# A decoder trunk: low weight parts built by an accumulating DMA, another order in the value product, a finer cut of the last columns

## The chip, the cores and the metric

The kernel runs on one core of a Trainium2 chip. The core has a tensor engine for matrix products (PE; its weight loads are shown apart as PEld), a vector engine (DVE), a scalar engine (ACT), GpSimd (POOL) and a sync engine (SP) that issues most DMAs. Matrix products read SBUF and write PSUM, eight banks of 128 x 512 fp32 each. The metric is the device time of one execution in microseconds (us).

## The reference

One layer (DEPTH = 1) on 512 tokens of width 1024. What matters here:

```python
h = rmsnorm(x, norm_mix_pre[l])
proj = h @ w_in[l]
...
y_b = swa_mixer(s_q, s_k, s_v, swa_sinks[l]) @ w_branch_swa[l]     # sliding-window attention, 128-token blocks
...
x = x + rmsnorm(merged @ w_out[l], norm_mix_post[l])
h = rmsnorm(x, norm_ffn_pre[l])
f = conv_ffn(h, ffn_w_up[l], ffn_conv_w[l], ffn_conv_b[l], ffn_w_down[l])
x = x + rmsnorm(f, norm_ffn_post[l])

def conv_ffn(h, w_up, conv_w, conv_b, w_down):
    ...                                            # up (1024 -> 2 x 2816), causal depthwise conv, split
    return (jax.nn.gelu(gate, approximate=True) * val) @ w_down     # 2816 -> 1024
```

In `swa_mixer` each block of 128 queries reads its own and the previous block of keys; the value product is `einsum('bnhgqk,bnkhd->bnqhgd', p / denom, vw)`.

## The kernel before, in words

**Split products.** Almost every product is done on pairs: each fp32 matrix is split into a high part, rounded to the reduced format fp32r, and a low part, what is left. A product is then three matmuls into the same PSUM bank: high x high, high x low, low x high. Weights are split on the core. `load_raw` (L62) brings 128 x 1024 fp32 (512 KB) into a buffer `raw` (two of them) by a DMA of SP; `split` (L67) makes `whi` by a rounding copy on ACT (L68) and `wlo = raw - whi` on DVE (L69). There are four buffers each for `whi` and `wlo`, used in turn, so the split of a weight waits until PE is done with the weight four places earlier. `weight_order` lists all weights in the order of use, and `weight` (L95) starts the load of the weight `AHEAD` = 2 places on whenever it hands one out.

**Order on the engines.** Dependencies between instructions, and the waits that follow, are worked out by the framework when the program is built. It also orders the instructions of each engine: a list scheduler goes through them by the order in which they were written, with times that it supposes for each, and takes an instruction written later where an earlier one would not be ready. So an engine's order in the trace can differ from the order in the code, and it is fixed before the run.

**The value product** (`swa_b`, L404). For each of the four blocks of queries, eight heads of probabilities are transposed on PE into two banks (`pt`, one for each half `hh` of four heads). In block 0 ACT copies them (L414). In blocks 1 to 3 DVE multiplies each bank by two masks (L419), which gives the products for the previous and the own block of keys. Then PE multiplies with the values (L426) into one bank `po`: half 0 to partitions 0 to 63, half 1 to partitions 64 to 127, with `n` = 1 (block 0) or 2 matmuls for each half. These are fp32 and show as two records each.

**The down product.** After the up products, `ah` and `al` hold the activations' parts, 22 chunks of 128 rows. The output is 4 token tiles x 2 column halves = 8 banks `pd[t][n]`, all open at once. For chunks 0 to 17 the loop runs over chunks, tiles and halves: `d_mm` (L836) issues three matmuls for each half, 24 for a chunk. The last four chunks (18 to 21) are loaded ahead, their weights held in all four buffers, and are done output by output: for each tile, for each half, the 12 matmuls of the four chunks. As each half is done, ACT squares it with a running sum (`jkf`, L856), and DVE multiplies it by the norm's gain (`fg`, L858). After the second half `rstd_m2` (L121) works out the inverse root from the sum, DVE adds the result to the residual `x1` (L865), and SP stores it (L867).

Of the kernel before, what the change touches and what calls it, by code (L numbers as in the profile page):

```python
# [7 lines left out]
F32 = mybir.dt.float32  # L8
F32R = mybir.dt.float32r
I32 = mybir.dt.int32  # L10
AF = mybir.ActivationFunctionType
ALU = mybir.AluOpType
AX = mybir.AxisListType

P = 128
T = 512
D = 1024
KC = D // P
NT = T // P
DFF = 2816  # L20
NF = DFF // P
EPS = 1e-6
VC = 656
# [27 lines left out]
def kernel(ctx: ExitStack, tc: tile.TileContext, x, xT, w_first, w_tiles, w_v, w_br, w_out, w_up, w_down,  # L51
                      pool_w, wgu, small, sinks, g_mix_post, g_ffn_pre, g_ffn_post,
                      ident_in, sel_in, tri_in, lvl_mask_in, scan_mask_in, pool_rc_in, out):
    nc = tc.nc
# [16 lines left out]
    def new_w():  # L71
        return (wp.tile([P, 1024], F32R, tag="whi", name="whi", bufs=4),
                wp.tile([P, 1024], F32R, tag="wlo", name="wlo", bufs=4))

    def load_w(src, cols=1024):
        raw = load_raw(src, cols)
        hi, lo = new_w()
        split(raw, hi, lo, slice(0, cols))
        return hi, lo
# [3 lines left out]
    loaded = {}  # L83
    pos = {"next": 0, "used": 0}

    def prefetch(upto):
        while pos["next"] < min(upto, len(order)):
            k = order[pos["next"]]
            src = tabs[k[0]]
            for i in k[1:]:  # L90
                src = src[i]
            loaded[k] = load_w(src, VC if k[0] == "v" else 1024)
            pos["next"] += 1

    def weight(*key, ahead=AHEAD):  # L95
# [39 lines left out]
    def base_of(pool, ssq, tag):  # L135
        b = pool.tile([P, 1], F32, tag=tag, name=tag, bufs=2)
        nc.vector.tensor_scalar(b, ssq, 1.0 / D, EPS, op0=ALU.mult, op1=ALU.add)
        return b
# [108 lines left out]
    with tc.tile_pool(name="mp", bufs=1) as mp:  # L247
# [77 lines left out]
        for i in range(4):  # L325
            qf_ = t2([P, T], f"swa_qf{i}")
            nc.vector.scalar_tensor_tensor(out=qf_, in0=pq[i], scalar=0.125, in1=rstd_b, op0=ALU.mult, op1=ALU.mult)
            for e in range(2):
                a, z = half[e], half[1 - e]
# [4 lines left out]
        for e in range(2):  # L334
            a, z = half[e], half[1 - e]
# [9 lines left out]
        for half in range(2):  # L345
            pv = [psm.tile([P, T], F32, tag="mm", name=f"pv{half}_{t}") for t in range(NT)]
            for k2 in range(4):
                hi, lo = weight("v", half * 4 + k2)
                for t in range(NT):
                    for kk in range(2):  # L350
                        kc = k2 * 2 + kk
                        c = slice(kk * 328, (kk + 1) * 328)
                        tk = slice(t * P, (t + 1) * P)
# [8 lines left out]
        def swa_steps():  # L362
            yh, yl = ybr[1] = new_y("y_swa")
            blk = {}
            nc.vector.tensor_scalar(nsink, sink, -1.0, None, op0=ALU.mult)

            def swa_a(b):
                s = t4([P, 8, P], f"s{b}")
                own = slice(b * P, (b + 1) * P)
                prev = slice((b - 1) * P, b * P)  # L370
                for hh in range(2):
                    for i2 in range(2):
                        sc = psx.tile([P, 2, 2, P], F32, tag="mx", name=f"sc{b}_{hh}_{i2}")
                        for ii in range(2):
                            q = qs[hh][:, i2 * 2 + ii, own]
                            if b:
                                kk = ks[:, hh, :, (b - 1) * P : (b + 1) * P]
                                nc.tensor.matmul(sc[:, ii, :, :], q, kk[:, 0, :], start=True, stop=False)
                                nc.tensor.matmul(sc[:, ii, :, :], q, kk[:, 1, :], start=False, stop=True)
                            else:  # L380
                                nc.tensor.matmul(sc[:, ii, 1, :], q, ks[:, hh, 0, own], start=True, stop=False)
                                nc.tensor.matmul(sc[:, ii, 1, :], q, ks[:, hh, 1, own], start=False, stop=True)
                        sv = s[:, hh * 4 + i2 * 2 : hh * 4 + i2 * 2 + 2, :]
                        nc.scalar.copy(sv, sc[:, :, 1, :])
                        nc.vector.copy_predicated(sv, sel.unsqueeze(1).to_broadcast([P, 2, P]),
                                                  sc[:, :, 0, :] if b else neg.unsqueeze(2).to_broadcast([P, 2, P]))
                mx = mp.tile([P, 8], F32, tag="mxs", name="mxs", bufs=2)
                nc.vector.tensor_reduce(out=mx, in_=s, op=ALU.max, axis=AX.X)
                nm = mp.tile([P, 8], F32, tag="nm", name="nm", bufs=2)
                nc.vector.scalar_tensor_tensor(out=nm, in0=mx, scalar=-1.0, in1=nsink, op0=ALU.mult, op1=ALU.min)  # L390
                es = mp.tile([P, 8], F32, tag="es", name="es", bufs=2)
                nc.vector.tensor_add(es, sink, nm)
                nc.scalar.activation(es, es, AF.Exp)
                den = mp.tile([P, 8], F32, tag="den", name="den", bufs=2)
                for h in range(8):
                    nc.scalar.activation(s[:, h, :], s[:, h, :], AF.Exp, bias=nm[:, h : h + 1], accum_out=den[:, h : h + 1])
                nc.vector.tensor_add(den, den, es)
                rd = mp.tile([P, 8], F32, tag="rd", name="rd", bufs=2)
                nc.vector.reciprocal(rd, den)
                for h in range(8):  # L400
                    nc.vector.tensor_scalar(s[:, h, :], s[:, h, :], rd[:, h : h + 1], None, op0=ALU.mult)
                blk[b] = s

            def swa_b(b):  # L404
                s = blk.pop(b)
                po = psx.tile([P, 4, P], F32, tag="mx", name=f"po{b}")
                pts = []
                for hh in range(2):
                    pt = psx.tile([P, 4, P], F32, tag="mx", name=f"pt{b}_{hh}")
                    for i in range(4):  # L410
                        nc.tensor.transpose(pt[:, i, :], s[:, hh * 4 + i, :], ident)
                    if b == 0:
                        own = t2([P, 4, P], f"pT{b}")
                        nc.scalar.copy(own, pt)  # L414
                        pts.append((own,))
                    else:
                        two = t4([P, 2, 4, P], f"pT{b}_{hh}")
                        for j in range(2):
                            nc.vector.tensor_tensor(out=two[:, j, :, :], in0=pt,  # L419
                                                    in1=tri[:, j, :].unsqueeze(1).to_broadcast([P, 4, P]), op=ALU.mult)  # L420
                        pts.append((two[:, 0, :, :], two[:, 1, :, :]))
                for hh in range(2):
                    n = len(pts[hh])
                    for j in range(n):
                        vb = vv[:, b - n + 1 + j, V_SV + hh * 64 : V_SV + hh * 64 + 64]
                        nc.tensor.matmul(po[hh * 64 : hh * 64 + 64, :, :], vb, pts[hh][j], start=j == 0, stop=j == n - 1)  # L426
                bs = slice(b * P, (b + 1) * P)
                nc.scalar.copy(yh[:, :, bs], po)
                nc.vector.tensor_sub(yl[:, :, bs], po, yh[:, :, bs].bitcast(F32))

            swa_a(0)
            yield
            for b in range(NT):
                if b + 1 < NT:
                    swa_a(b + 1)
                    yield
                swa_b(b)
                yield
# [357 lines left out]
    with tc.tile_pool(name="fp", bufs=1) as fp:  # L796
# [39 lines left out]
        def d_mm(t, kc, wh, wl, ns_=(0, 1)):  # L836
            tk = slice(t * P, (t + 1) * P)
            for n in ns_:
                ns = slice(n * T, (n + 1) * T)
                nc.tensor.matmul(pd[t][n], ah[:, kc, tk], wh[:, ns], start=kc == 0, stop=False)  # L840
                nc.tensor.matmul(pd[t][n], ah[:, kc, tk], wl[:, ns], start=False, stop=False)  # L841
                nc.tensor.matmul(pd[t][n], al[:, kc, tk], wh[:, ns], start=False, stop=kc == NF - 1)  # L842

        for kc in range(NF - 4):
            wh, wl = weight("d", kc)
            for t in range(NT):
                d_mm(t, kc, wh, wl)
        wd = [weight("d", kc) for kc in range(NF - 4, NF)]
        for t in range(NT):
            ssf = fp.tile([P, 2], F32, tag="ssf", name="ssf", bufs=2)  # L850
            fg = []
            for n in range(2):
                for kc in range(NF - 4, NF):
                    d_mm(t, kc, *wd[kc - NF + 4], ns_=(n,))
                jk = fp.tile([P, T], F32, tag="t0", name="jkf", bufs=3)
                nc.scalar.activation(jk, pd[t][n], AF.Square, accum_out=ssf[:, n : n + 1])  # L856
                fgn = fp.tile([P, T], F32, tag="fg", name="fg", bufs=2)
                nc.vector.tensor_mul(fgn, pd[t][n], gpost[:, n * T : (n + 1) * T])  # L858
                fg.append(fgn)
                if n == 0:  # L860
                    fb = base_of(fp, ssf[:, 0:1], "fb")
            rf = rstd_m2(fp, ssf[:, 1:2], "rf", fb)
            for n in range(2):
                ns = slice(n * T, (n + 1) * T)
                nc.vector.scalar_tensor_tensor(out=x1[:, t, ns], in0=fg[n], scalar=rf, in1=x1[:, t, ns],  # L865
                                               op0=ALU.mult, op1=ALU.add)
                nc.sync.dma_start(out[t, :, ns], x1[:, t, ns])  # L867


def _layout(inputs):  # L870
# [89 lines left out]
```

## Time and profile before

| | |
|---|---|
| three runs | 800.25, 800.38, 802.51 us; median 800.38 |
| the profiled execution | 802.75 us, its span 801.0 |
| TensorE clock granted, mean | 0.997 |
| PE busy | 791.3 us of the span |
| DVE, ACT, POOL busy | 462.2, 328.3, 32.9 us |
| matmuls of the down product (L840 to L842) | 528, from 674.3 to 794.3 us of the span |
| DMA | 81.02 MB, 101 GB/s over the span |

Times in a trace are counted from the start of the span. A timeline row has the start, the length, the engine, the line of the code, the operation, what it writes and reads, and in brackets how long the engine was idle before it and who ended that. Matmuls are pipelined: a row's 0.39 us is the time of one through the array, and the next one starts 0.23 us after it. A row of the DMA table ends with the median time from issue to landing. A row of the waits has the sum, the number of times and the longest.

### The profile page before, as it was taken

Reading aid. Unit: us, or ns where it says so; the run is one execution under the profiler, and the core shown is the slowest. Engines: PE = TensorE matmul, PEld = TensorE weight load, DVE = VectorE, ACT = ScalarE, POOL = GpSimd, SP = SyncE. Lnnn points to the kernel's source line nnn. Section 1 sums busy time; section 2 is a strip of 40 time slices with the busy share of each in tenths; the row PEclk is TensorE's granted clock in tenths of the full one; section 3 lists DMA queues with packets and bytes.
Section 4 is the critical chain, followed back from the end, with each engine's and each line's share of the span. In section 5 each row is a group of like instructions: output and inputs, shape, how many; then the busy total and the mean of one; then the engine's idle time right before and its main releaser. Section 6 shows DMA issues by size and latency. Waiting matters only on the chain.

```text
span 801.0 us, 9610 instructions
## 1 busy us (share of the span) xinstructions
PE 791.3 (99%) x3748; PEld 655.1 (82%) x3748; DVE 462.2 (58%) x701; ACT 328.3 (41%) x541; POOL 32.9 (4%) x46
## 2 busy tenths in 40 slices
PE   9999999999999999999999999999999999999996
PEld 7899876778887888888889988888888888888885
DVE  6464676368786556545658666655655665221225
ACT  7354644473224342333445544444444444122132
POOL 0100000011413000000000100000000000000000
PEclk9999999999999999999999999999999999999999
DMA  9434211122224213222550233223223223223202
GB/s 339 128 107 138 74 62 60 65 79 79 79 93 132 80 52 106 92 93 79 174 194 28 93 117 106 92 93 105 97 89 105 101 84 106 98 86 106 104 29 105
DMA packets 24781, 81.02 MB, mean 101 GB/s; under 512 B 2976, under 2 KB 3248, under 8 KB 24736
## 3 DMA queue, kind: packets, MB, share of 16 engines
q1 hardware_dynamic: 23760, 77.83, 27.9%
q0 software_dynamic: 832, 2.58, 1.0%
q8 instruction: 29, 0.48, 0.2%
q14 instruction: 16, 0.13, 0.1%
q10 hardware_dynamic: 144, 0.00, 0.0%
HBM read 78.30 MB, written 2.10 MB: 100 GB/s over the span
## 4 chain that ended last, share of the span: by engine, by line
PE 97%; DVE 1%; ACT 1%; issue 1%; DMA 0%; DVEq 0%
PE up L104 10%; PE up L102 10%; PE up L103 10%; PE pj L102 8%; PE pj L104 8%; PE pj L103 8%; PE pd L841 5%; PE pd L842 5%; PE pd L840 5%; PE pq L195 3%; PE py L104 3%; PE py L103 3%; PE py L102 3%; PE pz L723 2%; PE pz L725 2%; PE pz L724 2%
## 5 line engine op out<-in xcount | busy, mean ns | idle before, releaser
L69 DVE TENSOR_TENSOR wlo<-raw,whi 128x1024 fp32r<-128x1024 f32 (+1 forms) x127 | 152.3, 1201 | 201.4 <-ACT whi L68 201.2
L68 ACT CAST whi<-raw 128x1024 fp32r<-128x1024 f32 (+1 forms) x127 | 131.0, 1032 | 232.8 <-PE pj L103 77.9
L102 PE MATMUL up<-h_hi,whi 128*128 128x512 f32 (+1 forms) x384 | 142.8, 372 | 0.0
L103 PE MATMUL up<-h_lo,whi 128*128 128x512 f32 (+1 forms) x384 | 142.6, 371 | 0.0
L104 PE MATMUL up<-h_hi,wlo 128*128 128x512 f32 (+1 forms) x384 | 142.6, 371 | 0.0
L102 PE MATMUL pj<-h_hi,whi 128*128 128x512 f32 x296 | 117.8, 398 | 0.0
L104 PE MATMUL pj<-h_hi,wlo 128*128 128x512 f32 x296 | 116.2, 392 | 0.0
L103 PE MATMUL pj<-h_lo,whi 128*128 128x512 f32 x296 | 115.8, 391 | 0.0
L103 PEld LDWEIGHTS up<-h_lo,whi 128*128 128x128 f32 x384 | 72.3, 188 | 12.6
L104 PEld LDWEIGHTS up<-h_hi,wlo 128*128 128x128 f32 x384 | 72.3, 188 | 12.5
L102 PEld LDWEIGHTS up<-h_hi,whi 128*128 128x128 f32 x384 | 72.3, 188 | 12.3
L841 PE MATMUL pd<-wlo,act_hi 128*128 128x512 f32 x176 | 68.6, 390 | 0.0
L842 PE MATMUL pd<-whi,act_lo 128*128 128x512 f32 x176 | 68.5, 389 | 0.0
L840 PE MATMUL pd<-whi,act_hi 128*128 128x512 f32 x176 | 68.3, 389 | 0.0
L104 PEld LDWEIGHTS pj<-h_hi,wlo 128*128 128x128 f32 x296 | 55.6, 188 | 14.7 <-issue 2.6
L102 PEld LDWEIGHTS pj<-h_hi,whi 128*128 128x128 f32 x296 | 55.8, 188 | 13.4 <-issue 2.6
L103 PEld LDWEIGHTS pj<-h_lo,whi 128*128 128x128 f32 x296 | 55.8, 188 | 12.1 <-issue 1.0
L841 PEld LDWEIGHTS pd<-wlo,act_hi 128*128 128x128 f32 x176 | 33.0, 188 | 7.2 <-DVE wlo L69 0.3
L840 PEld LDWEIGHTS pd<-whi,act_hi 128*128 128x128 f32 x176 | 33.0, 188 | 6.9
L842 PEld LDWEIGHTS pd<-whi,act_lo 128*128 128x128 f32 x176 | 33.0, 188 | 6.7
L817 ACT CAST act_hi<-t 128x512 fp32r<-128x512 f32 x22 | 13.7, 621 | 58.6 <-DVE t L816 58.6
L805 ACT ACTIVATE t<-up,small_sb 128x512 f32<-128x512 f32 x44 | 34.0, 774 | 0.0
(272 smaller groups left out, 1087.7 us busy)
## 6 DMA issues: line engine op xcount, KB each, us to landing
raw<-in_w_up_dram SPq DMA_DIRECT2D x44, 512.0 KB, 3.2
raw<-in_w_tiles_dram SPq DMA_DIRECT2D x37, 512.0 KB, 3.2
raw<-in_w_down_dram SPq DMA_DIRECT2D x22, 512.0 KB, 3.2
raw<-in_w_br_dram SPq DMA_DIRECT2D x12, 512.0 KB, 3.3
raw<-in_w_out_dram SPq DMA_DIRECT2D x8, 512.0 KB, 3.3
raw<-in_w_v_dram SPq DMA_DIRECT2D x8, 328.0 KB, 3.1
xT<-in_xT_dram SPq DMA_DIRECT2D x8, 256.0 KB, 4.5
wfr<-in_w_first_dram SPq DMA_DIRECT2D x8, 256.0 KB, 4.3
```

Of the source, the lines that this page charges most:

```text
L68: nc.scalar.copy(hi[:, c], raw[:, c])
L69: nc.vector.tensor_sub(lo[:, c], raw[:, c], hi[:, c].bitcast(F32))
L102: nc.tensor.matmul(ps, lh, rh, start=first, stop=False)
L103: nc.tensor.matmul(ps, lh, rl, start=False, stop=False)
L104: nc.tensor.matmul(ps, ll, rh, start=False, stop=last)
L195: nc.tensor.matmul(pq[i], w[:, kc, i * P : (i + 1) * P], h[:, kc, :], start=kc == 0 and n == 0, stop=kc == KC - 1 and n == 2)
L723: nc.tensor.matmul(pz[t][n], mh[:, kc % 4, tk], wh[:, ns], start=kc == 0, stop=False)
L724: nc.tensor.matmul(pz[t][n], mh[:, kc % 4, tk], wl[:, ns], start=False, stop=False)
L805: nc.scalar.activation(t0, ps, AF.Identity, bias=col(C_CB + i), scale=col(C_CW + 2 * 44 + i))
L840: nc.tensor.matmul(pd[t][n], ah[:, kc, tk], wh[:, ns], start=kc == 0, stop=False)
L841: nc.tensor.matmul(pd[t][n], ah[:, kc, tk], wl[:, ns], start=False, stop=False)
L842: nc.tensor.matmul(pd[t][n], al[:, kc, tk], wh[:, ns], start=False, stop=kc == NF - 1)
```

## The change

Three edits. The 22 down weights go through a new `load_w_acc`: ACT makes the high part, then writes the negated weight, rounded, into `wlo`; a DMA of POOL then reads the weight a second time from memory and adds it onto `wlo`. The subtraction on DVE is gone for them. In `swa_b` the loops over `hh` and `j` change places. The tail of the down product becomes a function over pieces of columns, two halves for tiles 0 to 2, and for the last tile one half and two quarters; the running base of the sum is a chain over the pieces, and `fg` is one tile of 1024 columns.

```diff
+    def load_w_acc(src):
+        raw = load_raw(src)
+        hi, lo = new_w()
+        nc.scalar.copy(hi, raw)
+        nc.scalar.activation(lo, raw, AF.Copy, scale=-1.0)
+        nc.gpsimd.dma_start(lo, src, accum_op=ALU.add)
+        return hi, lo
...
-            loaded[k] = load_w(src, VC if k[0] == "v" else 1024)
+            loaded[k] = load_w_acc(src) if k[0] == "d" else load_w(src, VC if k[0] == "v" else 1024)
...
-                for hh in range(2):
-                    n = len(pts[hh])
-                    for j in range(n):
+                n = len(pts[0])
+                for j in range(n):
+                    for hh in range(2):
                         vb = vv[:, b - n + 1 + j, V_SV + hh * 64 : V_SV + hh * 64 + 64]
                         nc.tensor.matmul(po[hh * 64 : hh * 64 + 64, :, :], vb, pts[hh][j], start=j == 0, stop=j == n - 1)
...
-                nc.tensor.matmul(pd[t][n], al[:, kc, tk], wh[:, ns], start=False, stop=kc == NF - 1)
+                nc.tensor.matmul(pd[t][n], al[:, kc, tk], wh[:, ns], start=False, stop=False)
...
-        for t in range(NT):
-            ssf = fp.tile([P, 2], F32, tag="ssf", name="ssf", bufs=2)
-            fg = []
-            for n in range(2):
+        def tail(t, pieces):
+
+            ssf = fp.tile([P, 4], F32, tag="ssf", name="ssf", bufs=2)
+            fg = fp.tile([P, D], F32, tag="fg", name="fg", bufs=2)
+            base = None
+            for k, (c0, c1) in enumerate(pieces):
+                n, cs = c0 // T, slice(c0, c1)
+                ps = pd[t][n][:, c0 - n * T : c1 - n * T]
+                tk = slice(t * P, (t + 1) * P)
                 for kc in range(NF - 4, NF):
-                    d_mm(t, kc, *wd[kc - NF + 4], ns_=(n,))
+                    wh, wl = wd[kc - NF + 4]
+                    for a, w in ((ah, wh), (ah, wl), (al, wh)):
+                        nc.tensor.matmul(ps, a[:, kc, tk], w[:, cs], start=False,
+                                         stop=a is al and kc == NF - 1, skip_group_check=c0 % T > 0)
                 jk = fp.tile([P, T], F32, tag="t0", name="jkf", bufs=3)
-                nc.scalar.activation(jk, pd[t][n], AF.Square, accum_out=ssf[:, n : n + 1])
-                fgn = fp.tile([P, T], F32, tag="fg", name="fg", bufs=2)
-                nc.vector.tensor_mul(fgn, pd[t][n], gpost[:, n * T : (n + 1) * T])
-                fg.append(fgn)
-                if n == 0:
-                    fb = base_of(fp, ssf[:, 0:1], "fb")
-            rf = rstd_m2(fp, ssf[:, 1:2], "rf", fb)
+                nc.scalar.activation(jk[:, : c1 - c0], ps, AF.Square, accum_out=ssf[:, k : k + 1])
+                if k < len(pieces) - 1:
+                    b = fp.tile([P, 1], F32, tag="fb", name="fb", bufs=4)
+                    nc.vector.tensor_scalar(b, ssf[:, k : k + 1], 1.0 / D, EPS if base is None else base,
+                                            op0=ALU.mult, op1=ALU.add)
+                    base = b
+                nc.vector.tensor_mul(fg[:, cs], ps, gpost[:, cs])
+            rf = rstd_m2(fp, ssf[:, k : k + 1], "rf", base)
             for n in range(2):
                 ns = slice(n * T, (n + 1) * T)
-                nc.vector.scalar_tensor_tensor(out=x1[:, t, ns], in0=fg[n], scalar=rf, in1=x1[:, t, ns],
+                nc.vector.scalar_tensor_tensor(out=x1[:, t, ns], in0=fg[:, ns], scalar=rf, in1=x1[:, t, ns],
                                                op0=ALU.mult, op1=ALU.add)
                 nc.sync.dma_start(out[t, :, ns], x1[:, t, ns])
+
+        for t in range(NT):
+            tail(t, ((0, 512), (512, 1024)) if t < NT - 1 else ((0, 512), (512, 768), (768, 1024)))
```

## The prediction

> **What bounds the kernel now.** I read the engine totals of the page first, then its chain of work, then busy time by stage, then single instructions around the one place where the tensor engine (PE) waits in the changed code.
>
> ```profile
> span 801.0 us, 9610 instructions
> PE 791.3 (99%) x3748; PEld 655.1 (82%) x3748; DVE 462.2 (58%) x701; ACT 328.3 (41%) x541; POOL 32.9 (4%) x46
> PE 97%; DVE 1%; ACT 1%; issue 1%; DMA 0%; DVEq 0%
> 10.00:20.00 10.00, 10.00 (x44) 8.17 (x44) 7.03 (x10) 7.92 (x12) 0.00 (x0) 1.00 1.01 392
> 674.00:772.40 98.40, 98.40 (x435) 81.48 (x435) 24.84 (x22) 20.28 (x20) 0.00 (x0) 1.00 0.26 91
> 772.40:794.40 22.00, 21.94 (x96) 17.57 (x95) 12.14 (x30) 8.06 (x20) 0.00 (x0) 1.00 0.19 72
> 794.40:801.00 6.60, 0.00 (x0) 0.00 (x0) 2.67 (x7) 0.96 (x3) 0.00 (x0) 0.86 0.21 79
> ```
>
> The third line is the chain that ended last: 97% PE. In the stage rows (columns: length, busy us of PE, weight loads, DVE, ACT, POOL, then clock, DMA share, GB/s) PE is busy all of the down stage's 98.4 us, DVE for only 24.84, ACT for 20.28, POOL for none. So taking 22 DVE subtractions away frees an engine that nothing waits for: it is worth nothing by itself. What counts is when a low weight part (wlo) is ready for PE, and the last 6.6 us, in which PE has nothing left.
>
> ```profile
> 756.09 1.05 ACT L68 CAST whi<-raw 128x1024 fp32r<-128x1024 f32 x1 [4.38 <-PE pd L842]
> ...
> 766.97 1.05 ACT L68 CAST whi<-raw 128x1024 fp32r<-128x1024 f32 x1 [4.38 <-PE pd L842]
> 772.41 1.05 ACT L68 CAST whi<-raw 128x1024 fp32r<-128x1024 f32 x1 [4.38 <-PE pd L842]
> 773.50 1.23 DVE L69 TENSOR_TENSOR wlo<-raw,whi 128x1024 fp32r<-128x1024 f32 x1 [4.22 <-ACT whi L68]
> 774.02 0.39 PE L842 MATMUL pd<-whi,act_lo 128*128 128x512 f32 x1
> 774.25 0.61 PE L840 MATMUL pd<-whi,act_hi 128*128 128x512 f32 x2
> 774.78 0.50 PE L841 MATMUL pd<-wlo,act_hi 128*128 128x512 f32 x1
> 775.11 0.39 PE L842 MATMUL pd<-whi,act_lo 128*128 128x512 f32 x1
> 775.34 0.40 PE L841 MATMUL pd<-wlo,act_hi 128*128 128x512 f32 x1
> PEld pd L841 <- DVE wlo L69: 0.3, 1, 0.3
> ```
>
> The casts come 5.44 us apart (766.97 to 772.41), each let go by the matmul that ends the use of the buffer four weights earlier. So PE spends 5.44 us on a weight, 24 matmuls of 0.227, and a cast starts three weights, 16.3 us, ahead of its use. The last weight (chunk 21) is the exception. The tail takes the first 512 columns of chunks 18 to 21 at once, so it wants wlo of chunk 21 after ten matmuls, at 774.47 if nothing waits (two steps of 0.227 after the 774.02 row), 2.1 us after its buffer came free at 772.4. Cast and subtraction take until 774.73, and PE waits 0.3 us, the stage's only wait. Two L840 stand in a row at 774.25, though one output takes L840, L841, L842 in turn: the second belongs to the other output, pulled forward into the gap. The order on an engine is thus not the written one; a scheduler fills a gap that it foresees. From 774.25 to 775.34 four steps took 1.09 us instead of 0.91: the wait costs 0.18.
>
> **The low parts by an accumulating DMA.** Removed: 22 DVE subtractions of 1.23 us. Added: 22 ACT instructions, 22 POOL issues, 22 transfers of 512 KB.
>
> ```profile
> L762 ACT ACTIVATE hn<-x 128x1024 f32<-128x1024 f32 x4 | 4.2, 1061 | 3.7 <-DVE x L757 3.6
> raw<-in_w_down_dram SPq DMA_DIRECT2D x22, 512.0 KB, 3.2
> x<-in_x_dram SPq DMA_DIRECT2D x4, 512.0 KB, 7.7
> 443.07 0.59 POOL L800 DMA_DIRECT2D g_ffn_post<-in_g_ffn_post_dram  x1 [193.04 <-ACT h_hi L773]
> 447.12 2.76 POOL L801 TENSOR_SCALAR g_ffn_post<-g_ffn_post 128x1024 f32<-128x1024 f32 x1 [3.46 <-DMA g_ffn_post<-in_g_ffn_post_dram]
> ```
>
> A scaled ACT copy of 1024 columns takes 1.06 us (L762's size), 22 x 1.06 = 23.3 us on an ACT that is 80% idle in the stage. A plain 512 KB transfer issued by POOL lands 447.12 - 443.07 = 4.05 us after its issue begins, the 0.59 of descriptor work included. No row shows an accumulating one. From below it is bounded by 4.05 (it must also read the tile that it adds to; nothing lets it move less), from above by the 7.7 us that 512 KB took on the full DMA of the start (x). I take the plain time and one more 512 KB of engine time: the stage's 0.26 share x 5.44 us = 1.41 us for each weight, so 4.05 + 1.41 = 5.46, nearest to the uncontended POOL row, since the stage leaves 74% of the DMA free.
>
> The Trainium skill, "Collectives: The Full Stack", section "The bandwidth ceiling: the fold count and why AG ≠ RS ≠ AR", says that an add in the DMA is slowed by its two source reads and not by the adding; by it the transfer part would about double. No run here shows that yet.
>
> Steady weights: cast 1.05, activation 1.06 and transfer 5.46 make 7.6 us (9.8 by the upper bound) against a lead of 16.3, so nothing; the cover goes only where a transfer takes over 14.2 us. The queues: ACT has only these in the stage; POOL has no work of its own there, so an accumulate that waits for ACT holds up only later ones; SP's next raw load waits for the second ACT read instead of the subtraction, 2.1 us instead of 2.3 after the cast began. DMA share: 0.26 now, 0.52 with a transfer priced as a raw one, 0.78 at double.
>
> The last weight is where it hurts. Its chain starts at 772.41 as before: 772.41 + 1.05 + 1.06 = 774.52, landing at 778.6 (plain), 780.0 (taken), 782.2 (upper). In written order PE wants it at 774.47. Chunk 20 has 5.44 us more and is wanted 0.68 sooner: hidden behind the same lateness. So wlo comes 5.5 us late (4.1 to 7.7). There is work for that gap: seven other outputs, each with ten matmuls that don't need this wlo, 70 x 0.227 = 15.9 us. Total PE work doesn't change, so what is filled costs nothing. How much is filled depends on the time that the scheduler supposes, which no row gives; ends are all and nothing. I take a gap planned for a plain transfer, since the 774.25 row shows lateness planned within one matmul: filled 4.1, left 1.41. **Cost +1.4 - 0.18 = +1.2 us** (0 - 0.18 to +7.5).
>
> **The last columns.** The last output's second half is cut into 256 + 256.
>
> ```profile
> 98.99 0.28 PE L378 MATMUL sc<-swa_k,swa_q 128*128 128x256 f32 x1
> ...
> 99.22 0.28 PE L378 MATMUL sc<-swa_k,swa_q 128*128 128x256 f32 x1
> L396 ACT ACTIVATE s<-s,nm 128x128 f32<-128x128 f32 x32 | 12.4, 389 | 7.8 <-DVE nm L390 7.8
> L856 ACT ACTIVATE jkf<-pd 128x512 f32<-128x512 f32 x8 | 4.8, 599 | 13.8 <-PE pd L842 13.8
> L858 DVE TENSOR_TENSOR fg<-pd,g_ffn_post 128x512 f32<-128x512 f32 x8 | 5.5, 690 | 8.3 <-ACT jkf L856 8.3
> L69 DVE TENSOR_TENSOR wlo<-raw,whi 128x1024 fp32r<-128x1024 f32 x119 | 145.8, 1225 | 192.1 <-ACT whi L68 191.9
> 795.10 0.69 DVE L858 TENSOR_TENSOR fg<-pd,g_ffn_post 128x512 f32<-128x512 f32 x1 [1.97 <-ACT jkf L856]
> 796.46 1.42 DVE L865 SCALAR_TENSOR_TENSOR x<-fg,rfr,x 128x512 f32<-128x512 f32 x2
> ```
>
> Matmuls of 256 columns start 0.115 us apart: 24 x 0.115 instead of 12 x 0.227 is +0.04. The last one takes 0.28 instead of 0.39: -0.11. The square on 256 columns saves 256 x (599 - 389)/384 ns = 0.14. The product saves (1225 - 690)/2 = 0.27. All stand in a row ahead of 796.46; what follows is unchanged. The first half's extra base and product run beside the second half's 1.4 us of matmuls. **-0.48 us**; bounds -0.5 and 0 (the square's fixed part could eat it).
>
> **The value product.** The order on two output halves changes from 0,0,1,1 to 0,1,0,1 in blocks 1 to 3; block 0 is the same.
>
> ```profile
> 95.92 1.41 PE po L426 x4
> 108.12 2.15 PE po L426 x6
> 112.99 1.00 PE po L426 x2
> 107.19 1.28 DVE L419 TENSOR_TENSOR pT<-pt,tri 128x512 f32<-128x512 f32 x2
> 108.46 0.68 DVE L419 TENSOR_TENSOR pT<-pt,tri 128x512 f32<-128x512 f32 x1
> 111.30 0.68 DVE L419 TENSOR_TENSOR pT<-pt,tri 128x512 f32<-128x512 f32 x1
> ```
>
> Each matmul is two records. Two records take 1.00 us, four that change halves once take 1.41, not 2: records of different halves overlap. More changes of half could overlap more. But the inputs decide: both inputs of half 0 are ready at 108.47, the first of half 1 at 109.14, the second at 111.98, and PE started that one only at 112.99, with other work between. When the first product ends (about 108.12 + 0.86 = 108.98), half 1 isn't ready and half 0's second input is, so the scheduler would choose the old order again. **0**, bounds -1.00 x 3 = -3.0 (the fourth product wholly overlapped) and +0.16 x 3 = +0.5 (PE waits from 108.98 to 109.14).
>
> **Sum.** 802.75 (the profiled execution) + 1.4 - 0.18 - 0.48 + 0 = 803.5. That execution lies 2.37 above the median, so I apply the difference, +0.74, to 800.38: **801.1 us**. What this measurement can tell from no change is 0.3%, 2.4 us: 798.0 to 802.8.
>
> **The rivals.**
> PE waits in full: the order isn't refilled, or for a much shorter time. For it: only one matmul was pulled forward so far. Against it: that was as much as was needed. Cost 4.1 to 5.5, less 0.66: 803.8 to 805.2. In the last stage row the granted clock averages 0.86 over 6.6 us without matmuls, so a long wait may also leave PE slow for some us, to 807. The Trainium skill, "TensorE: Matmul & The Clock Gate", Part 1, says that about 3.4 us idle bring the clock to half for as long again, an estimate of 1.7 us more here; the first matmul-free stretch that a trace of this case shows is the end.
>
> The accumulating transfer is slow in bulk. Beside a raw load's 1.41 us it must stay under 5.44 - 1.41 = 4.03 us of all engines, 2.9 plain ones; at four plain ones a weight takes 7.05 us, 22 x 1.6 = 35 us more, 836. The quiet 74% of the DMA speaks against it, the missing row leaves it open.
>
> Faster: PE's order changes in all three blocks, the fourth product overlaps each time, and the scheduler fills the last gap: 800.38 - 3.0 - 0.66 = 796.7. It decides from 1.8 us of gain on. Against it: the late fourth input, at 111.98.
>
> **How the numbers follow.** The forecast with its own range 799.7 (all filled) to 802.8: 0.48. Full wait: 0.22. The same mechanism with a remainder over 2.4 us after a slower transfer (about 804): 0.06. Bulk-bound: 0.09. Faster: 0.15. So faster 0.15, same 0.48, slower 0.37. The range 797.0 to 807.0 leaves out the bulk case and the best of the faster one.
>
> **What would show it.** Right: PE matmuls of other outputs between 774.4 and the landing of the last wlo, a wait of PE on a DMA of 1 to 2 us there and none at the other weights; DVE without L69 in the stage; PE's last matmul to the end about 0.5 us shorter; the product still in groups of 6 and 2. Wrong: PE waiting at every weight, a DMA share over 0.9 in the stage, or landings over 14 us after the issue; a single wait over 3 us with a clock below 1; or groups of 8 records.

## The result, and the profile after

The changed kernel took 804.0 us (median of 10 runs, 803.05 to 805.67), the kernel before 802.01 beside it on the same chip (10 runs, 800.25 to 802.63): a ratio of 1.0032, 95% interval 1.0022 to 1.0041. It is slower by about as much as this measurement can tell at all. The executions of the kernels that ran often fall in groups 1.6 to 1.9 us apart (before: near 798.7, 800.4 and 802.2), so besides the ratio I give the difference between like groups; for the change that is +2.9 us. Where that isn't enough, I count within a profiled execution from the end of the first product's 96 matmuls to the last instruction: 770.9 us before, 773.5 after, +2.6. Below, "profiled" with a signed number stands for this difference to the kernel before.

The profiled execution took 804.66 us. The head of its page, and below it the busy time by stage (length, busy us of PE, weight loads, DVE, ACT, POOL, then clock, DMA share, GB/s):

```profile
span 802.9 us, 9669 instructions
PE 790.9 (99%) x3760; PEld 654.5 (82%) x3760; DVE 435.6 (54%) x681; ACT 349.3 (44%) x565; POOL 52.1 (6%) x68
...
raw<-in_w_down_dram SPq DMA_DIRECT2D x22, 512.0 KB, 6.1
wlo<-in_w_down_dram POOLq DMA_DIRECT2D x22, 512.0 KB, 6.7
```

```profile
674.00:772.40 98.40, 98.40 (x436) 81.51 (x435) 2.88 (x4) 37.71 (x40) 15.68 (x18) 1.00 0.85 194
772.40:794.40 22.00, 19.87 (x92) 16.01 (x90) 10.82 (x29) 8.13 (x21) 0.87 (x1) 1.00 0.30 87
794.40:803.00 8.60, 1.69 (x12) 1.49 (x12) 2.95 (x9) 0.78 (x4) 0.00 (x0) 0.89 0.22 83
```

In the down stage DVE fell from 24.84 us to 2.88, ACT rose from 20.28 to 37.71, and PE is busy for all 98.40 us as before. The DMA share rose from 0.26 to 0.85. Nearly everything that the change did to the time comes after 772.4: there PE is busy for 19.87 of 22.00 us (21.94 before). The waits of PE's weight loads say where (us in total, times, longest):

```profile
PEld pd L869 <- DMA wlo<-in_w_down_dram: 2.0, 1, 2.0
PEld pd L869 <- DVE fg L878: 1.3, 1, 1.3
...
```

Two waits that count, each once. The first, in the timeline of the last weight (chunk 21):

```profile
771.19 1.06 ACT L79 ACTIVATE wlo<-raw 128x1024 fp32r<-128x1024 f32 x1 [3.44 <-PE pd L849]
771.22 0.39 PE L869 MATMUL pd<-whi,act_hi 128*128 128x512 f32 x1
...
772.16 1.03 ACT L78 CAST whi<-raw 128x1024 fp32r<-128x1024 f32 x1
...
772.54 0.87 POOL L80 DMA_DIRECT2D wlo<-in_w_down_dram  x1 [4.57 <-ACT wlo L79]
...
773.26 0.71 PE L869 MATMUL pd<-whi,act_hi 128*128 128x512 f32 x2
773.81 0.39 PE L869 MATMUL pd<-wlo,act_hi 128*128 128x512 f32 x1
...
775.64 0.39 PE L869 MATMUL pd<-whi,act_hi 128*128 128x512 f32 x1
777.66 0.50 PE L869 MATMUL pd<-wlo,act_hi 128*128 128x512 f32 x1 [1.63 <-DMA wlo<-in_w_down_dram]
778.00 0.39 PE L869 MATMUL pd<-whi,act_lo 128*128 128x512 f32 x1
```

ACT makes the negated copy first, then the cast. POOL issues the transfer at 772.54, and PE gets its result at 777.6, 5.06 us later. Ten matmuls after 771.22 PE would want it, at 773.49, so it is 4.1 us late. PE does ten matmuls of another output in that time, from the second one of the pair at 773.26 to 775.64, and then stands. From 775.87 to 777.66 is 1.8 us, and the first matmul after it costs 0.1 more.

The second wait, in the timeline of the last output (the first quarter's last matmul, DVE's product on it, the second quarter's first and last matmul):

```profile
793.62 0.28 PE L869 MATMUL pd<-whi,act_lo 128*128 128x256 f32 x1
794.57 0.41 DVE L878 TENSOR_TENSOR fg<-pd,g_ffn_post 128x256 f32<-128x256 f32 x1
795.04 0.38 PE L869 MATMUL pd<-whi,act_hi 128*128 128x256 f32 x1 [1.15 <-DVE fg L878]
...
796.46 0.28 PE L869 MATMUL pd<-whi,act_lo 128*128 128x256 f32 x1
```

The second quarter's columns are other columns than the first's, but they lie in the same PSUM tile and bank. PE doesn't start on them until ACT's square and DVE's product have read the first quarter: 1.3 us, and 0.1 for the restart. Before, the last matmul was this one:

```profile
793.95 0.39 PE L842 MATMUL pd<-whi,act_lo 128*128 128x512 f32 x1
```

From the start of the last matmul to the end of the span there are now 802.9 - 796.46 = 6.44 us, before 801.0 - 793.95 = 7.05: the shorter ending came, 0.61 us of it, and the wait ahead of it took more than twice that.

### The profile page after: what moved, and what is told of

Read it like the earlier page. It is cut to its first block, busy times and chain, and to the rows that moved or that the text cites. A ratio compares the mean times of both kernels' runs of the same rounds, so it can differ in the third digit from the quotient of the medians.

```text
span 802.9 us, 9669 instructions
## 1 busy us (share of the span) xinstructions
PE 790.9 (99%) x3760; PEld 654.5 (82%) x3760; DVE 435.6 (54%) x681; ACT 349.3 (44%) x565; POOL 52.1 (6%) x68
## 4 chain that ended last, share of the span: by engine, by line
PE 84%; issue 11%; POOL 2%; DVE 1%; DMA 1%; ACT 1%; DVEq 0%; POOLq 0%
PE up L110 10%; PE up L111 10%; PE up L112 10%; PE pj L112 8%; PE pj L110 8%; PE pj L111 8%; PE pq L203 3%; PE py L112 3%; PE py L111 3%; PE py L110 3%; PE pd L869 2%; POOL wlo L80 2%; PE pz L731 2%; PE pz L733 2%; PE pz L732 2%
## 5 line engine op out<-in xcount | busy, mean ns | idle before, releaser
L69 DVE TENSOR_TENSOR wlo<-raw,whi 128x1024 fp32r<-128x1024 f32 (+1 forms) x105 | 125.3, 1196 | 121.6 <-ACT whi L68 121.4
L68 ACT CAST whi<-raw 128x1024 fp32r<-128x1024 f32 (+1 forms) x105 | 107.8, 1027 | 153.1 <-PE pj L111 76.1
L848 PE MATMUL pd<-whi,act_hi 128*128 128x512 f32 x144 | 56.0, 389 | 0.0
L850 PE MATMUL pd<-whi,act_lo 128*128 128x512 f32 x144 | 56.0, 389 | 0.0
L849 PE MATMUL pd<-wlo,act_hi 128*128 128x512 f32 x144 | 56.0, 389 | 0.0
L79 ACT ACTIVATE wlo<-raw 128x1024 fp32r<-128x1024 f32 x22 | 23.3, 1059 | 59.3 <-PE pd L849 55.7
L80 POOL DMA_DIRECT2D wlo<-in_w_down_dram x22 | 19.2, 874 | 305.4 <-ACT wlo L79 305.4
L814 DVE SCALAR_TENSOR_TENSOR t<-up,small_sb,t 128x511 f32<-128x511 f32 x44 | 32.7, 744 | 11.3 <-ACT t L813 11.3
```

The costliest lines, as they stand in the source:

```text
L68: nc.scalar.copy(hi[:, c], raw[:, c])
L69: nc.vector.tensor_sub(lo[:, c], raw[:, c], hi[:, c].bitcast(F32))
L79: nc.scalar.activation(lo, raw, AF.Copy, scale=-1.0)
L80: nc.gpsimd.dma_start(lo, src, accum_op=ALU.add)
L814: nc.vector.scalar_tensor_tensor(out=t0[:, 1:], in0=ps[:, : T - 1], scalar=col(C_CW + 44 + i), in1=t0[:, 1:], op0=ALU.mult, op1=ALU.add)
```

## The experiments

Three kernels do one part of the change each, on the kernel before.

**The accumulating transfer alone.**

```diff
-            loaded[k] = load_w(src, VC if k[0] == "v" else 1024)
+            loaded[k] = load_w_acc(src) if k[0] == "d" else load_w(src, VC if k[0] == "v" else 1024)
```

> The kernel before with the accumulating DMA for the 22 down weights and nothing else of the change. Theory A (the last weight's low part lands about 1.9 us after PE has run out of pulled-forward matmuls, the other 21 are hidden): +1.7 to +1.9 us on before, ratio 1.0022, one PE wait on a DMA of about 2 us at chunk 21, none elsewhere. Rival B (the loaded DMA engines, 0.85 of the stage, cost the whole of the slowdown): +2.9 us, ratio 1.0036, with several PE or ACT waits spread over the stage.

802.61 us, ratio 1.0024 (1.0014 to 1.0035); like groups +2.05, profiled +2.1. PE's waits in the down stage:

```profile
PEld pd L849 <- DMA wlo<-in_w_down_dram: 2.4, 1, 2.4
```

One wait at the last weight and no other on a transfer: the 22 accumulates cost what the last one costs.

**The last columns alone** (the changed kernel's tail, with the low parts made by DVE as before).

```diff
+        for t in range(NT):
+            tail(t, ((0, 512), (512, 1024)) if t < NT - 1 else ((0, 512), (512, 768), (768, 1024)))
```

> The kernel before with the new tail (last half in two quarters) and nothing else. Theory A (the second quarter's first matmul waits until DVE has read the first quarter, because both lie in one bank): the shorter ending gives -0.6, 24 matmuls at 0.12 instead of 12 at 0.227 cost +0.16, the wait costs +1.4: +0.95 us, ratio 1.0012, with a PE wait of 1.2 to 1.4 us on fg. The prediction's step: -0.48 us, ratio 0.9994, no wait.

803.12 us, ratio 1.002 (1.0008 to 1.0033); like groups +1.0, profiled +1.0. The prediction had -0.48.

```profile
PEld pd L869 <- DVE fg L878: 1.3, 1, 1.3
PEld pd L869 <- DVE wlo L69: 0.3, 1, 0.3
```

The new wait on DVE's product stands beside the old 0.3 us on the subtraction, so it has nothing to do with the transfers.

**The value product's loops alone.**

```diff
-                for hh in range(2):
-                    n = len(pts[hh])
-                    for j in range(n):
+                n = len(pts[0])
+                for j in range(n):
+                    for hh in range(2):
```

> The kernel before with the two loops of the value product exchanged and nothing else. Theory A (the four product groups take 0.1 us less, the extra gaps give it back): -0.1 us, ratio 0.9999. Rival (the exchange gives the 1 us by which PE reached the tail earlier in the profiled run of the changed kernel): -1.0 us, ratio 0.9988.

800.32 us, ratio 0.9998 (0.9985 to 1.001); like groups -0.1, profiled -0.2. The three single edits add up to 2.1 + 1.0 - 0.2 = +2.9 against +2.6 for the whole change. They hardly touch each other; the 0.3 us between the sums is about what one wait differs by: the weight loads wait 2.4 us for the last transfer with the transfers alone, and 2.0 in the whole change.

**Is it the shared bank?** The changed kernel with the last output's pieces in another order: a quarter, then the 512 columns of the other bank, then the other quarter. DVE reads the first quarter while PE works elsewhere.

```diff
-            tail(t, ... else ((0, 512), (512, 768), (768, 1024)))
+            tail(t, ... else ((512, 768), (0, 512), (768, 1024)))
```

> The changed kernel with the last tile's pieces in the order (512 to 768), (0 to 512), (768 to 1024), so that 2.7 us of matmuls on the other bank lie between the two quarters of one bank. Theory A (a wait on the shared bank): the wait on fg is gone, 1.3 to 1.4 us less than the changed kernel: +1.5 us on before, ratio 1.0019. Rival C (the quarters cost by their small matmuls and extra steps, not by the wait): as the changed kernel, +2.9 us, ratio 1.0036.

803.68 us, ratio 1.0027 (1.0015 to 1.0038); like groups +1.6, profiled +2.0. The wait on DVE is gone:

```profile
PEld pd L869 <- DMA wlo<-in_w_down_dram: 2.6, 1, 2.6
```

The same matmuls in the same sizes, only apart in time, don't wait. So the 1.3 us come from PE's writing next to a piece that is still being read, not from the cut itself. The Trainium skill, "PSUM — Partial Sum Buffer", section "PSUM bank collisions raise a hardware error", says that an engine's write and another's read of one bank have to be kept apart even at different columns, by bank (and group of 32 partitions) and not by address; the wait agrees with that. Whether it is the tile or the bank by which this program keeps them apart, no run here shows.

**Is it the last weight only?** The changed kernel, with the low part of chunk 21 made by DVE as before.

```diff
-            loaded[k] = load_w_acc(src) if k[0] == "d" else ...
+            loaded[k] = load_w_acc(src) if k[0] == "d" and k[1] < NF - 1 else ...
```

> The changed kernel, but chunk 21 alone split as before (raw load, cast, subtraction on DVE); chunks 0 to 20 keep the accumulating DMA. Theory A (only the last weight's transfer is waited for): the PE wait on a DMA is gone, no other takes its place; 1.8 to 2.0 us less than the changed kernel: +1.0 us on before, ratio 1.0012, as with the new tail alone. Rival (chunk 20 is late as well, or the loaded DMA engines cost by themselves): +2 us or more.

801.46 us, ratio 1.0009 (0.9998 to 1.0021); like groups +1.0, profiled +1.1.

```profile
PEld pd L869 <- DMA wlo<-in_w_down_dram: 0.6, 1, 0.6
```

The 2.0 us are gone, and the wait on DVE's product stands as before, 1.3 us. A 0.6 us wait of the weight loads for the weight before the last is left, which the last one's lateness had covered.

**Both repairs**: the changed kernel with all low parts by DVE and the pieces apart; what stays of the change is the swapped loops and the shorter ending.

```diff
-            loaded[k] = load_w_acc(src) if k[0] == "d" else load_w(src, ...)
+            loaded[k] = load_w(src, VC if k[0] == "v" else 1024)
...
+            tail(t, ... else ((512, 768), (0, 512), (768, 1024)))
```

> The changed kernel without the accumulating DMA (all weights split as before) and with the last tile's pieces in the order (512 to 768), (0 to 512), (768 to 1024). Theory A (the two waits are all that the change lost, the shorter ending of 0.6 us stays, 0.16 goes to the quarters): -0.4 to -0.6 us on before, ratio 0.9994, last matmul to the end 6.4 us instead of 7.0. Rival (the quarters cost more than the ending gives): 0 to +0.5 us.

799.99 us, ratio 0.9992 (0.9981 to 1.0003); like groups -0.4. It is the best of the versions, and its interval doesn't part it from the kernel before.

**What makes the transfer long?** The changed kernel, with POOL's transfer as a plain one: the adding is left out, all else stays.

```diff
-        nc.gpsimd.dma_start(lo, src, accum_op=ALU.add)
+        nc.gpsimd.dma_start(lo, src)
```

> The changed kernel with a plain transfer of POOL in place of the accumulating one: the adding is left out, the low part holds the whole weight. Theory A (the second read and the add are what makes the transfer long): it lands in 4.0 to 4.5 us instead of 5 to 6.7, the issue on POOL takes 0.55 instead of 0.87 us, the DMA share of the stage is 0.52 instead of 0.85, and PE's wait for the last one is about 1.0 us shorter. Rival (a transfer issued by POOL is long of itself, with or without the add): lands in 5 us or more, share 0.8.

801.82 us, ratio 1.0014 (1.0001 to 1.0027); like groups +1.5. The stage row, the transfers, and the wait at the last weights:

```profile
674.00:772.40 98.40, 98.40 (x435) 81.32 (x434) 0.76 (x2) 36.55 (x37) 9.49 (x18) 1.00 0.56 192
```

```profile
raw<-in_w_down_dram SPq DMA_DIRECT2D x22, 512.0 KB, 4.4
wlo<-in_w_down_dram POOLq DMA_DIRECT2D x22, 512.0 KB, 3.8
```

```profile
PEld pd L869 <- DMA wlo<-in_w_down_dram: 0.6, 1, 0.6
```

The same bytes written, 192 GB/s against 194, but a DMA share of 0.56 instead of 0.85, a landing after 3.8 us instead of 6.7, and raw loads of 4.4 instead of 6.1 beside them. The last weight comes nearly in time. So the length is the adding's; whether by the second read that it needs or by the sum itself, this run doesn't part.

**How near is the DMA to its end?** Four kernels; the first three didn't settle it. First, a second accumulate into the same tile (which leaves wlo with the weight added once too often).

```diff
         nc.gpsimd.dma_start(lo, src, accum_op=ALU.add)
+        nc.gpsimd.dma_start(lo, src, accum_op=ALU.add)
```

> The changed kernel with two accumulating DMAs for each down weight, one behind the other: the weight is added once too often. The share of the DMA engines in the stage went from 0.26 to 0.85 with one, 0.59 x 5.44 = 3.2 us of all engines for each weight, so two and the raw load would need 1.44 x 5.44 = 7.8 us against PE's 5.44. Theory A (DMA time is the bound that one transfer stays just under): the stage becomes bound by the DMA, 22 x 2.4 = 52 us less what the first weights are ahead, 840 us or more, PE waiting at most weights. Rival (the share overstates it, much of it is waiting time of the queues): only the last weight is later, by 5 to 6 us: about 809 us.

877.67 us, ratio 1.0952 (1.0921 to 1.0982), PE waiting at every weight. But the DMA isn't full, and POOL's timeline (brackets: idle time before, and what ended it) shows another bound:

```profile
674.00:772.40 98.40, 74.92 (x280) 57.53 (x281) 2.88 (x4) 24.67 (x26) 20.45 (x24) 0.91 0.86 189
```

```profile
713.61 0.87 POOL L81 DMA_DIRECT2D wlo<-in_w_down_dram  x1 [6.48 <-DMA wlo<-in_w_down_dram]
714.14 1.24 POOL L80 DMA_DIRECT2D wlo<-in_w_down_dram  x1
721.88 0.87 POOL L81 DMA_DIRECT2D wlo<-in_w_down_dram  x1 [6.49 <-DMA wlo<-in_w_down_dram]
```

The second accumulate waits 6.5 us for the first, and the next weight's issue is queued behind it on POOL: one weight for each 8.27 us. That is a chain, not a full DMA; the number above the expected 840 says nothing for bandwidth.

So the second accumulate went into two spare tiles that nobody reads.

```diff
         nc.gpsimd.dma_start(lo, src, accum_op=ALU.add)
+        nc.gpsimd.dma_start(spare[pos["next"] % 2], src, accum_op=ALU.add)
```

> The changed kernel with a second accumulating transfer of 512 KB for each down weight, into two spare tiles that nobody reads, so that no weight waits for it. Theory (the DMA engines' time decides): with 3.2 us of engine time for each accumulate and 1.41 for the raw load, a weight takes 1.41 + 6.4 = 7.8 us instead of 5.44; 22 x 2.4 = 52 us, less the 16.3 us of lead: 840 to 856, PE waiting for wlo at most weights, DMA share in the stage at 0.9 or above. Rival (the slowness of two accumulates into one tile was the chain of the second on the first, on POOL's queue): 804 to 810, the share higher than 0.85 without PE waiting at more than the last weights.

804.83 us, ratio 1.0033 (1.0017 to 1.0049), as the changed kernel. It didn't test what it was made for: with nothing to hold them back, the 22 spare transfers were issued from 444 to 528 us, in the stage before. There they show something else:

```profile
444.00:529.00 85.00, 85.00 (x424) 72.46 (x424) 54.18 (x65) 39.91 (x51) 22.55 (x24) 1.00 0.99 231
```

The DMA is full there (0.99; 0.30 without them), the accumulates come 84/21 = 4.0 us apart, and PE is still busy for all 85 us. Each spare transfer from the third on has to wait until the one two before it, into the same tile, has landed.

To hold them in the down stage, ACT first copied one column of raw into the spare tile.

```diff
+        sp = spare[pos["next"] % 2]
+        nc.scalar.copy(sp[:, 0:1], raw[:, 0:1])
+        nc.gpsimd.dma_start(sp, src, accum_op=ALU.add)
```

> The changed kernel with a second accumulating transfer of 512 KB beside each down weight's own, into one of two spare tiles that nobody reads; ACT first copies one column of raw into the spare tile, so that the transfer stays in the down stage. It isn't chained to the weight's own transfer by data. Theory (the DMA engines' time decides): accumulates that ran alone beside raw loads, with the DMA share at 1.01, came 4.0 us apart; two for each weight are 8.0 us of pace against 5.44, 22 x 2.6 = 56 us less a lead of 11 to 16 us: 843 to 865, the share in the stage at 0.95 or above, PE waiting on wlo at most weights. Rival (two accumulates into one tile were slow because the second waited for the first on POOL's queue): 804 to 815, PE waiting only at the last weights.

883.79 us, ratio 1.1025 (1.097 to 1.108), and again not by the DMA, whose share was 0.79 in the stage. ACT's timeline:

```profile
720.55 0.19 ACT L82 COPY spare<-raw 128x1 f32<-128x1 f32 x1 [8.00 <-DMA raw<-in_w_down_dram]
...
721.61 1.03 ACT L78 CAST whi<-raw 128x1024 fp32r<-128x1024 f32 x1
731.06 0.19 ACT L82 COPY spare<-raw 128x1 f32<-128x1 f32 x1 [8.43 <-DMA raw<-in_w_down_dram]
```

In the program ACT's small copy of the next weight's raw stands ahead of the cast of this one. So the cast that frees a raw buffer waits for the next raw load, and one load was in flight instead of two: 10.5 us for a weight. My probe had added a wait of its own.

Reading the column from the high part instead puts it behind its own weight's cast.

```diff
-        nc.scalar.copy(sp[:, 0:1], raw[:, 0:1])
+        nc.scalar.copy(sp[:, 0:1], hi[:, 0:1].bitcast(F32))
```

> As the run before with the late spare transfers, but the one-column copy reads the high part, so that ACT does it after the cast of its own weight and doesn't wait for the next raw load ahead of it (that order had left one raw load in flight). Again two accumulating transfers of 512 KB for each down weight, one of them into a spare tile that nobody reads. Theory (the DMA engines' time decides): two accumulates at the 4.0 us pace measured with the DMA full, 8.0 us for a weight against 5.44: 22 x 2.6 = 56 us less 11 to 16 us of lead: 843 to 860, DMA share in the stage 0.95 or above. Rival (only chains of waits made the two kernels with twice the accumulates slow): 804 to 815, PE waiting at the last weights only.

824.77 us, ratio 1.029 (1.0189 to 1.0391). Stage row, PE's waits, and POOL's issues for wlo:

```profile
674.00:772.40 98.40, 92.15 (x393) 72.45 (x391) 2.37 (x4) 33.96 (x50) 27.84 (x32) 1.00 1.06 251
```

```profile
PEld pd L856 <- DMA wlo<-in_w_down_dram: 12.1, 13, 1.2
PEld pd L876 <- DMA wlo<-in_w_down_dram: 9.4, 3, 4.5
```

```profile
690.48 0.87 POOL L80 DMA_DIRECT2D wlo<-in_w_down_dram  x1
...
772.58 0.87 POOL L80 DMA_DIRECT2D wlo<-in_w_down_dram  x1
```

The DMA share is 1.06 now, and PE waits for a transfer at 13 steady weights and three times in the tail. 13 steps from 690.48 to 772.58 are 6.32 us for a weight. If the DMA alone sets this pace, then with the raw load's 1.41 an accumulate is worth (6.32 - 1.41)/2 = 2.46 us of all DMA engines. But a chain is left here too, in ACT's timeline:

```profile
720.89 0.19 ACT L82 COPY spare<-whi 128x1 f32<-128x1 f32 x1 [4.20 <-DMA spare<-in_w_down_dram]
```

At each weight ACT's small copy waits until the spare transfer of two weights before has landed. That takes 12.0 us, and the weight's own accumulate 14.7 (medians) where the changed kernel's took 6.7, so the chain is long because the DMA is loaded; how much of the 6.32 us is the chain's, no run here parts. So 2.46 us is an upper estimate.

The theory held in kind. The rival (804 to 815, PE waiting only at the last weights) missed the time, but it isn't ruled out that a chain gave part of it. The theory's 843 to 860 was too high, because the 4.0 us of the early spare transfers already held the raw loads of their stage. Worked out from those: 231 GB/s x 4.0 us are 0.92 MB, 0.40 more than the accumulate's 0.52, and at 1.41 us for each 0.52 they took 1.1, which leaves 2.9, an upper estimate for the same reason. So an accumulate is worth at most 2.5 to 2.9 us, 1.7 to 2.1 times a raw load. The Trainium skill, "Collectives: The Full Stack", section "The bandwidth ceiling: the fold count and why AG ≠ RS ≠ AR", puts the cost of an add in the DMA, there in a ReduceScatter, down to its two source reads, about a doubling; these rows agree with the size, and that the reads are the cause no run here shows.

**Would halves land sooner?** The changed kernel, with each accumulate in two halves of the columns.

```diff
-        nc.gpsimd.dma_start(lo, src, accum_op=ALU.add)
+        for c in (slice(0, 512), slice(512, 1024)):
+            nc.gpsimd.dma_start(lo[:, c], src[:, c], accum_op=ALU.add)
```

> The changed kernel with the accumulating transfer in two, columns 0 to 511 first, each with its own issue. The first half moves half the bytes. Theory (the last weight's wait is the time from its buffer's release to the landing, and moved bytes are a part of it): first half lands 1 to 2 us earlier, PE's wait on the DMA falls from 2.0 to 0.5 to 1.5 us, time 0.5 to 1.5 below the changed kernel. Rival (fixed cost of an issue and a landing rules, 0.9 us of POOL for each): the wait stays at 2 us or grows, and the steady weights still hide all, time 0 to +0.5.

805.13 us, ratio 1.0044 (1.0026 to 1.0061): no gain, as the rival had it.

```profile
PEld pd L870 <- DMA wlo<-in_w_down_dram: 2.7, 2, 2.0
```

PE waits for each half. The first one was there 4.2 us after its issue instead of 5.06, but the order on PE held only six matmuls for the gap instead of ten.

## Why the prediction was right or wrong

The time, 804.0, lies in the range and 2.9 us above the forecast of 801.1; against the before of its own runs the change cost 2.0 by the medians and 2.6 by the profiles, where the prediction had +0.74. That the range held is its width, 10 us, and not the sum: the accumulate was 0.9 us dearer than forecast, the last columns 1.5, and 0.5 came back from the loops (0.2) and from the parts together (0.3). The forecast was a change under the 0.3% that this measurement can tell; the measured 0.32% lies just on that line. Point by point:

- **DVE's subtractions worth nothing, steady weights hidden: right.** PE's 98.40 of 98.40 us didn't change, and no steady weight waited. The accumulates landed 5.1 to 9.4 us after their issue (median 6.7), far from the 14.2 at which the cover would go.
- **The accumulate's price: inside its bounds.** I took 5.46 us (4.05 to 7.7) for the landing; the last weight's was 5.06. The share was expected at 0.52 or 0.78 and was 0.85, above both. With 2.46 us for an accumulate the stage would need 3.9 of each 5.44 us, 0.71, so the share isn't the need alone; what the rest is, no run shows.
- **The last weight: the mechanism right, its two sizes wrong, both ways.** The wait was foreseen at 1.4 us and cost 1.9, and the transfers alone cost 2.1 where +1.2 was foreseen. The low part came 4.1 us late instead of 5.5. Of the 1.4 us, 1.0 is the scheduler's, which let ACT write the negated copy first, at 771.19, where the chain that I had drawn began with the cast; 0.4 is the shorter landing. But PE's order held 2.3 us of other work (ten matmuls) instead of 4.1. That order is fixed before anything runs, so the scheduler must have supposed a shorter transfer than the real one; the time that it supposed stands in no row. It is the step that I had called unknown, with ends at all and nothing; I chose too much.
- **The last columns: wrong, the step that failed.** "The first half's extra base and product run beside the second half's 1.4 us of matmuls" took for granted that the matmuls run on beside a read of their neighbours in the same tile. They waited 1.3 us for it. The rest of the step was right: 0.61 us at the ending against the 0.52 that stands behind its -0.48, and a quarter's matmuls 0.12 us apart. So +1.0 instead of -0.48, 1.5 us of the miss of 1.9 (2.6 against 0.74); its bounds, -0.5 and 0, had no room for it because I looked for a new wait only at the transfers.
- **The value product: the size right, the reason wrong.** The scheduler did change the order. The chain of work shows it after, as count and length of the product's parts:

```profile
107.29 1.00 PE po L434 x2
108.95 1.01 PE po L434 x4
112.23 1.00 PE po L434 x2
...
134.72 1.00 PE po L434 x2
136.39 1.86 PE po L434 x6
```

  Instead of six records and two there are two, four and two in blocks 1 and 2 (half 0's first product, other work, then one of each half, then half 1's last) and two and six in block 3. In blocks 1 and 2 the last product still comes after the late fourth input, as the prediction had argued. In block 3 DVE made the four inputs in one row, and the product ended as long after the last of them as before (2.0 us). So little came of it (-0.1 to -0.2).
- **The rivals.** The time falls into the 803.8 to 805.2 of "PE waits in full", but its mechanism didn't happen: PE filled the gap with ten matmuls, and the rest of the time is the wait at the last columns. Without the kernel that does only the last columns I'd have taken one for the other. The prediction also took the end of the trace for its first matmul-free stretch; in the kernel before there is one at 167.5, of 0.97 us, which with sixteen matmuls of two columns in 1.92 us behind it is followed by 3.41 us at half clock, from 171.07. The slow bulk didn't come: an accumulate is worth at most 2.5 to 2.9 us of the DMA, under the 4.03 that stood as its threshold; with two for each weight PE did wait (824.77). The faster end needed the fourth product to overlap, and it didn't.

## What to carry to other kernels

Before an output is cut into finer pieces to shorten the ending, look at what reads each piece and whether the next one's matmuls write the same PSUM tile, here a whole bank: put work on another one between them, or the cut can cost the time of those reads (here 1.4 us for 0.6 gained). Work moved from an idle engine to the DMA gains nothing where PE is the bound, and costs at the last item, where the lead is gone; keep that one on the short path. In a probe that adds work, look at the order it gave the engines before reading its time: two of mine measured mainly the chains that they had made, and a third has one in its pace.

## What the runs showed of the hardware

Short waits can bring the tensor engine's clock to half, but the length of a wait alone doesn't decide it. In the kernel with two accumulates into one tile, PE stands once for each weight; two of its waits and what follows:

```profile
718.87 0.50 PE L850 MATMUL pd<-wlo,act_hi 128*128 128x512 f32 x1 [2.23 <-DMA wlo<-in_w_down_dram]
...
719.84 0.63 PE L850 MATMUL pd<-wlo,act_hi 128*128 128x512 f32 x1
...
722.83 0.43 PE L851 MATMUL pd<-whi,act_lo 128*128 128x512 f32 x1
...
768.64 0.50 PE L850 MATMUL pd<-wlo,act_hi 128*128 128x512 f32 x1 [2.35 <-DMA wlo<-in_w_down_dram]
768.98 0.39 PE L851 MATMUL pd<-whi,act_lo 128*128 128x512 f32 x1
769.21 0.40 PE L849 MATMUL pd<-whi,act_hi 128*128 128x512 f32 x1
```

After 2.23 us without matmuls the granted clock is 0.50 for 3.41 us, from 719.46 to 722.87, and the matmuls come 0.43 us apart instead of 0.23. After 2.35 us it is 1.00, and they come 0.23 apart. The 1.63 us of the changed kernel and the 2.22 us of the one with the pieces apart left the clock at 1.00 as well. In the kernel with two accumulates the half clock begins at 702.40, 719.46 and 736.53, among others, steps of 17.1 us or five times 3.41, while the waits before it end at 702.57, 718.87 and 735.66. What decides at these lengths is open. The Trainium skill, "TensorE: Matmul & The Clock Gate", Part 1, gives an idle window of about 3.4 us as what brings the half clock: the length of the slow time agrees, but here 2.23 us of idling were enough in one place, and 2.35 us were not in another.

In the profiled executions, the difference between the groups of times lies in two places that the change doesn't touch. The first product's 96 matmuls took 22.0 to 24.3 us in different executions, and around 170 us the granted clock differed, after the same matmuls and the same 1 us of idling; the stage rows there of the kernel before and of the one with both repairs:

```profile
170.00:175.00 5.00, 5.00 (x18) 4.00 (x18) 3.19 (x5) 4.39 (x15) 0.00 (x0) 0.66 0.34 108
```

```profile
170.00:175.00 5.00, 5.00 (x24) 4.13 (x23) 2.14 (x4) 4.22 (x12) 0.00 (x0) 1.00 0.32 108
```

At 0.66 PE starts 18 matmuls in those 5 us, at 1.00 it starts 24; over that stretch the executions differ by 1.6 us, which is a group's distance.
